# The output projection of each layer as one group of seven products

## The chip, the cores and the metric

The kernel runs on one core of a Trainium2 chip. The metric is the device time of one launch, in microseconds (us); the time given is the median of several runs.

## The reference, cut to what matters

Two layers of a hybrid decoder, on one sequence of 512 tokens with 1024 channels, all in float32. Each layer is a feed-forward, a mixer and a second feed-forward:

```python
for l in range(2):
    x = x + 0.5 * swiglu(rms_norm(x, ffn1_norm[l]), ffn1_wg[l], ffn1_wu[l], ffn1_wd[l])
    z = rms_norm(x, mix_norm[l]) @ w_in[l]       # q | k | v | conv_B | conv_C | conv_h
    attn_out = sliding_window_attention(q, k, v, sink[l])               # 512 channels
    conv_out = conv_B * causal_conv3(conv_C * conv_h, conv_w[l])        # 512 channels
    x = x + concat([attn_out, conv_out]) @ w_out[l]                     # 1024 x 1024
    x = x + 0.5 * swiglu(rms_norm(x, ffn2_norm[l]), ffn2_wg[l], ffn2_wu[l], ffn2_wd[l])
return rms_norm(x, final_norm)
```

The line with `w_out` is the output projection.

## The kernel before

The activations x lie in SBUF with channels on the partitions: eight tiles `xs[c]` of 128 channels by 512 tokens, in pairs `xpair` (the trace calls them x). TensorE (PE) multiplies in a rounded 32-bit form (`F32R`), so each operand is split into a rounded first part and a second part with the rest: `split` (lines 198 and 199) casts on ScalarE (ACT) and subtracts on VectorE (DVE). Each product is then three matmuls: first by first, first by second, second by first.

Weights come through one stream. `plan` writes out all units and the order of their use; `need_raw` loads units four ahead, through the queue of SyncE (SP), into 8 buffers `raw`; `need_split` splits them two ahead into 3 buffers `wh` and 3 buffers `wl`. A split marked "far" (lines 236 to 238) makes the second part without VectorE: ScalarE writes the negated rounded copy and the rounded copy, and a DMA issued by GpSimd (POOL) adds the raw tile to the negated copy. The scheduler of the language puts the instructions of each engine in order; each engine then works through its own in that order, and one that waits holds up all behind it.

Two ways to multiply are used:

- `group` (lines 258 to 276): a plain product, one tile of 128 output channels, 8 k-tiles with three matmuls of 512 columns each, 24 in all. The output projection uses eight of them, in `mix` (lines 1278 to 1281). After each, VectorE adds the result to `xs[c]`, and `after(c)` prepares the next norm for that tile: `take` makes its two parts (xh, xl), `square` adds to the sum of squares (nacc).
- groups of seven (Strassen's scheme in Winograd's form): a product of 2 by 2 blocks by seven products of half the size. The forms of the weights are a11, a12, s2, s3, s1, a22, s4; the operands are b11, b21, t2, t3, t1, t4, b22 in the order of `CHAINS`. `Seven.make` makes an operand (sums t1 to t4 on VectorE, then a split); `share` runs the seven products for a down projection, with `stand`, whose matmuls have 256 columns, and adds each result to the quarters of x that it belongs to (`SHARES`). Of the weight sums, s1 and s3 start in DRAM: a second load, issued by POOL, adds to the first as it lands (line 193). s2 is added on VectorE (line 217), and for units marked "share" s4 = a12 + s2 is a DMA issued by POOL (line 243). At the end of a feed-forward the last `share` calls `into.step` after each product, which calls `take_half` for that quarter of x, the counterpart of `take`.

The mixer (`mix`) runs 18 plain groups of `w_in` with the norm factored out; between them `attend(step)` puts the stages of eight attention units (two groups of heads by four blocks of 128 tokens): scores, transposes, values. The convolution multiplies on POOL, the last time `cb` by y. The outputs are split at once into the projection's operands `m`: for attention by ScalarE and POOL, for the convolution by ScalarE and VectorE.

Behind the mixer the second feed-forward begins with `plain`: four plain groups, with the inverse root of the norm worked out in the second (`factors`), then a small down projection, then blocks of seven products (`winograd2`, matmuls in `stream`).

Of the kernel before, what the change touches and what calls it, by code (L numbers as in the profile page):

```python
# [15 lines left out]
P = 128  # L16
# [42 lines left out]
def trunk_kernel(  # L59
# [32 lines left out]
    def psum(tag, shape, name):  # L92
        return ps.tile(shape, F32, tag=tag, bufs={"mm": 4, "sc": 2, "aux": 2}[tag], name=name)
# [21 lines left out]
    def f32(ap):  # L115
        return ap.bitcast(F32)
# [177 lines left out]
    def plan():  # L294
        def cols(src, k0, kc, n, how=None):
            wide = abreast(kc)
            for b in range(0, n, wide):
                order.append((add_unit((src, k0, kc, b * P, wide * P)), how))
# [349 lines left out]
    def make_bias():  # L648
# [9 lines left out]
        for h in range(NH):  # L658
            nc.vector.scalar_tensor_tensor(
                bias[:, h, :], df, -(2.0 ** -(h + 1)), m0, op0=ALU.mult, op1=ALU.add  # L660
            )


    def ffn(norm, stages, after=None, late=None):

# [167 lines left out]

            pending.extend(lambda *tag, c=c: turn(c, *tag) for c in range(NT))

        def stand(accs, wh, wl, xh, xl, h, start):

            for c in range(4):
                cols = slice(c * P, (c + 1) * P)
                for k in range(2):  # L840
                    for i, (w, x_) in enumerate(((wh, xh), (wh, xl), (wl, xh))):

                        nc.tensor.matmul(  # L843
                            accs[c // 2][:, c % 2, :],
                            w[:, k, cols],
                            x_[:, 2 * h + k, :],
                            start=start and c % 2 == 0 and h + k + i == 0,
                            stop=h + k == 2 and i == 2,
                            skip_group_check=True,
                        )  # L850

        def stream(accs, wh, wl, xh, xl, h, start):

            for u in range(2):
                tok = slice(u * P, (u + 1) * P)
                for k in range(2):
                    for i, (x_, w) in enumerate(((xh, wh), (xl, wh), (xh, wl))):
                        nc.tensor.matmul(  # L858
                            accs[u],
                            x_[:, 2 * h + k, tok],  # L860
                            w[:, k, :],
                            start=start and h + k + i == 0,
                            stop=h + k == 2 and i == 2,
                            skip_group_check=not start,
                        )

        def share(b, ops, between, y=None):


            accs = {}  # L870
            for step, (acc, operand, start) in enumerate(CHAINS):
                ops.make(operand)
                xh, xl = ops.forms[operand]
                if start:
                    tag = {"x": "mm", "y": "sc", "w": "aux"}[acc]
                    shape = [P, 2, H] if y is None else [P, S]
                    accs[acc] = [psum(tag, shape, f"{acc}_{ops.name}_{m}") for m in range(2)]
                o, t, sign = SHARES[step]
                for h in range(2):
                    _, wh, wl = take_split()  # L880
                    if y is None:
                        stand(accs[acc], wh, wl, xh, xl, h, start)
                    else:
                        stream(accs[acc], wh, wl, xh, xl, h, start)
                    if h == 0:
                        continue
                    for m in range(2):
                        if y is None:
                            part = xpair[2 * o + m][:, :, t * H : (t + 1) * H]
                        else:  # L890
                            part = y[2 * t + m][o]
                        nc.vector.scalar_tensor_tensor(
                            part, accs[acc][m], 0.5 * sign, part, op0=ALU.mult, op1=ALU.add
                        )
                if step < 3:
                    ops.make(CHAINS[step + 4][1])
                between(step)

        def shared(b):
            return Seven([raws[b], raws[b + 2]], room_form, f"s_{norm.i}_{b}")  # L900

        def turns(step):
# [2 lines left out]
                flush()  # L905
            if step == 2:
                flush(2, "mm")

        def ahead(ops, at):
            return lambda step: ops.make(*at.get(step, ()))  # L910

        sevens = [b for what, b in stages if what == "s"]
        blocks = [b + j for b in sevens for j in (0, 2)]
# [9 lines left out]
        for i, (what, b) in enumerate(stages):  # L923
            if what in "wu" and stages[i + 1][0] == "s":
                ops = shared(sevens[0])
                if what == "w":
                    winograd2(b, ahead(ops, {3: ("b11",), 4: ("b21",), 5: ("t2",), 6: ("t3",)}))
                else:
                    winograd(b, ahead(ops, {1: ("b11",), 2: ("b21",), 4: ("t2",), 6: ("t3",)}))
            elif what == "w":  # L930
                if after is None and b == 1:
                    end = Finale()
                winograd2(b, end and b == 1 and end.step)
            if what == "s" and b == sevens[0]:
                then = shared(sevens[1])
                share(
                    b,
                    ops,
                    ahead(then, {3: ("b11",), 4: ("b21",), 5: ("t2",), 6: ("t3",)}),
                    end and end.y,  # L940
                )
            elif what == "s" and i + 1 == len(stages):
                share(b, then, after.step)
            elif what == "s":
                share(b, then, lambda step: 2 <= step < 6 and flush(1, "aux"), end and end.y)
# [24 lines left out]
            if b == (1,) and late:  # L970
                late()
# [123 lines left out]


    def mix(l, norm, after):
        mixed = [None] * KC
        q = [None] * NH

        def scaled(acc, name, by=None):
            t = g2(name)
# [11 lines left out]
        for g in range(NKV):  # L1114
# [27 lines left out]
        class Unit:  # L1142
# [61 lines left out]
            def values(self):  # L1204
# [7 lines left out]
                    nc.tensor.matmul(o, v, lo, start=False, stop=i == len(self.pt) - 1)  # L1212
# [12 lines left out]

# [21 lines left out]
        for pair in range(2):  # L1247
# [6 lines left out]
            for j in range(2):  # L1254
# [11 lines left out]
                ys.append(y)  # L1266
                attend(step)
                step += 1
            hi, lo = parts_of(f"m_{l}_{2 + pair}")
            for j in range(2):  # L1270
                b = scaled(group(norm.h), f"cb_{l}_{pair}_{j}")
                nc.gpsimd.tensor_mul(b, b, ys[j])
                nc.scalar.copy(hi[:, j, :], b)
                nc.vector.tensor_sub(lo[:, j, :], b, f32(hi[:, j, :]))
# [63 lines left out]
```

## Time and profile before

| | |
|---|---|
| time, median of 3 runs | 1692.62 us (1692.27 to 1692.71) |
| the profiled execution | 1692.13 us, of it span 1690.3 us |
| mean granted TensorE clock | 0.999 |
| output projection, layer 0 | 470.2 to 513.7 us of the span |
| output projection, layer 1 | 1304.9 to 1348.5 us |

In the rows of the profile the engines are PE (matmuls), PEld (weight loads), DVE, ACT, POOL and SPq or POOLq for queues; "out<-in" names the tiles, L and a number is the line of the kernel, a bracket at the end is the idle time before an instruction and what ended it. A row of the timeline begins with the start in us from the start of the span and the length in us.

### The profile page before, as it was taken

What the parts mean: (1) busy time and instruction counts of PE and PEld (TensorE: products, weight loads), DVE (VectorE), ACT (ScalarE), POOL (GpSimd) and SP (SyncE); (2) the same over time, 40 slices, a digit from 0 to 9 for tenths busy, and PEclk for the clock granted to TensorE, in tenths of its full rate; (3) what the DMA queues carried; (4) which work ended last, traced back from release to release, by engine and by line L of the source; (5) the groups of instructions that cost most, each with busy time, mean ns of one, the idle gap of its engine ahead of it and who ended that gap; (6) DMA issues with size and microseconds to landing.
All of it is one profiled execution on the core that took longest, in us unless ns stands there. A gap on an engine that the chain in (4) does not pass through costs nothing.

```text
span 1690.3 us, 22800 instructions
## 1 busy us (share of the span) xinstructions
PE 1680.5 (99%) x8726; PEld 1434.4 (85%) x8726; DVE 1345.3 (80%) x1751; ACT 942.3 (56%) x1309; POOL 209.5 (12%) x190
## 2 busy tenths in 40 slices
PE   9999999999999999999999999999999999999998
PEld 6888899988888888889988888999888888888886
DVE  7987679988858976799798777997787597667995
ACT  6545565466535655564465555644565466556654
POOL 1011111001211111111011111110023011111111
PEclk9999999999999999999999999999999999999999
DMA  8467777731337677778576777794223457777881
GB/s 250 104 170 190 185 198 184 191 100 51 112 102 154 172 183 182 186 195 209 163 150 170 191 185 184 192 224 139 62 63 114 112 124 192 184 185 185 222 215 50
DMA packets 197600, 271.53 MB, mean 161 GB/s; under 512 B 8620, under 2 KB 91636, under 8 KB 197492
## 3 DMA queue, kind: packets, MB, share of 16 engines
q1 hardware_dynamic: 162308, 197.85, 37.5%
q0 software_dynamic: 34032, 70.79, 24.7%
q8 instruction: 68, 1.11, 0.3%
q10 hardware_dynamic: 1152, 1.45, 0.2%
q14 instruction: 40, 0.33, 0.1%
HBM read 254.85 MB, written 2.10 MB: 152 GB/s over the span
## 4 chain that ended last, share of the span: by engine, by line
PE 96%; DVE 2%; ACT 1%; DMA 0%; issue 0%; SPq 0%; ACTq 0%; DVEq 0%
PE x L858 24%; PE y L858 12%; PE acc L271 9%; PE acc L268 9%; PE acc L275 9%; PE x_s L843 8%; PE w L858 6%; PE y_s L843 4%; PE x_s L858 3%; PE w_s L843 2%; PE at L823 2%; PE y_s L858 1%; PE x L737 1%; PE w_s L858 1%; PE pt L1197 1%; DVE p L1190 0%
## 5 line engine op out<-in xcount | busy, mean ns | idle before, releaser
L198 ACT CAST wh<-raw 128x1024 fp32r<-128x1024 f32 (+1 forms) x472 | 494.7, 1048 | 552.7 <-PE x L858 134.2
L199 DVE TENSOR_TENSOR wl<-raw,wh 128x1024 fp32r<-128x1024 f32 (+1 forms) x471 | 578.5, 1229 | 214.5 <-ACT wh L198 212.5
L268 PE MATMUL acc<-xh,wh 128*128 128x512 f32 x448 | 176.5, 394 | 0.1
L271 PE MATMUL acc<-xl,wh 128*128 128x512 f32 x448 | 175.2, 391 | 0.1
L275 PE MATMUL acc<-xh,wl 128*128 128x512 f32 x416 | 162.4, 390 | 0.0
L193 POOL DMA_DIRECT2D raw<-in_ffn_wu_dram x39 | 47.3, 1217 | 569.1 <-DMA raw<-in_ffn_wu_dram 402.1
L271 PEld LDWEIGHTS acc<-xl,wh 128*128 128x128 f32 x448 | 84.2, 188 | 18.3 <-DVE xl L396 1.6
L268 PEld LDWEIGHTS acc<-xh,wh 128*128 128x128 f32 x448 | 84.2, 188 | 17.4 <-issue 0.5
L275 PEld LDWEIGHTS acc<-xh,wl 128*128 128x128 f32 x416 | 78.1, 188 | 16.3
L193 POOL DMA_DIRECT2D raw<-in_ffn_wg_dram x39 | 47.1, 1220 | 218.2 <-DMA raw<-in_ffn_wu_dram 70.9
L193 POOL DMA_DIRECT2D raw<-in_ffn_wd_dram x32 | 38.5, 1204 | 265.7 <-DMA raw<-in_ffn_wd_dram 144.8
L217 DVE TENSOR_TENSOR raw<-raw,raw 128x1024 f32<-128x1024 f32 x54 | 65.6, 1220 | 1.7 <-DMA raw<-in_ffn_wu_dram 1.0
L858 PE MATMUL w<-wh,fb21h 128*128 128x512 f32 x152 | 60.7, 399 | 0.0
L858 PE MATMUL x<-wh,ft2h 128*128 128x512 f32 x152 | 60.6, 398 | 0.0
L858 PE MATMUL y<-wh,ft3h 128*128 128x512 f32 x152 | 60.4, 398 | 0.0
L858 PE MATMUL w<-wl,fb21h 128*128 128x512 f32 x152 | 59.4, 391 | 0.0
L858 PE MATMUL x<-wl,ft2h 128*128 128x512 f32 x152 | 59.3, 390 | 0.0
L858 PE MATMUL y<-wh,ft3l 128*128 128x512 f32 x152 | 59.2, 390 | 0.0
L858 PE MATMUL y<-wl,ft3h 128*128 128x512 f32 x152 | 59.2, 390 | 0.0
L858 PE MATMUL w<-wh,fb21l 128*128 128x512 f32 x152 | 59.2, 389 | 0.0
L858 PE MATMUL x<-wl,fb11h 128*128 128x512 f32 x152 | 59.2, 389 | 0.0
L858 PE MATMUL x<-wh,fb11l 128*128 128x512 f32 x152 | 59.1, 389 | 0.0
(440 smaller groups left out, 4656.9 us busy)
## 6 DMA issues: line engine op xcount, KB each, us to landing
raw<-in_ffn_wu_dram SPq DMA_DIRECT2D x127, 512.0 KB, 4.0
raw<-in_ffn_wd_dram SPq DMA_DIRECT2D x104, 512.0 KB, 5.1
raw<-in_ffn_wg_dram SPq DMA_DIRECT2D x87, 512.0 KB, 4.5
raw<-in_ffn_wu_dram POOLq DMA_DIRECT2D x39, 512.0 KB, 7.9
raw<-in_ffn_wg_dram POOLq DMA_DIRECT2D x39, 512.0 KB, 5.9
raw<-in_w_in_dram SPq DMA_DIRECT2D x36, 512.0 KB, 3.7
raw<-in_ffn_wd_dram POOLq DMA_DIRECT2D x32, 512.0 KB, 8.1
raw<-raw POOLq DMA_DIRECT2D x16, 512.0 KB, 6.9
```

The costliest lines, as they stand in the source:

```text
L193: nc.gpsimd.dma_start(out=r, in_=rows_of(*more), accum_op=ALU.add)
L198: nc.scalar.copy(hi, raw)
L199: eng.tensor_sub(lo, raw, f32(hi))
L217: nc.vector.tensor_add(a11, a11, s1)
L268: nc.tensor.matmul(acc, hi[:, k, :], rhs[k][0], start=k == first, stop=False)
L271: nc.tensor.matmul(acc, hi[:, k, :], rhs[k][1], start=False, stop=n == 0 and k == last)
L275: nc.tensor.matmul(acc, lo[:, k, :], rhs[k][0], start=False, stop=k == last)
L737: nc.tensor.matmul(out, w[:, k, cols], x_[:, k, :], start=start and k + i == 0, stop=k == KC // 2 - 1 and i == 2, skip_group_check=not start,)
L823: nc.tensor.transpose(tp[:, t * P : (t + 1) * P], ups[t][:, c * P : (c + 1) * P], ident)
L843: nc.tensor.matmul(accs[c // 2][:, c % 2, :], w[:, k, cols], x_[:, 2 * h + k, :], start=start and c % 2 == 0 and h + k + i == 0, stop=h + ...
L858: nc.tensor.matmul(accs[u], x_[:, 2 * h + k, tok], w[:, k, :], start=start and h + k + i == 0, stop=h + k == 2 and i == 2, skip_group_chec ...
L1197: nc.tensor.transpose(tp[:, h, :], self.p[:, h, kb * P : (kb + 1) * P], ident)
```

## The change

`plan` puts `w_out` in as a group of seven instead of eight column units. Its tiles are marked "share", the very first "far". `stand`, `stream`, `share` and `ahead` move out of `ffn` unchanged but for two arguments of `share`: the factor `by` (0.5 in the feed-forwards, 1.0 here), and `soon`, with which the operand of the product after next is made ahead of the additions onto x. In `mix` the attention and the convolution write their outputs unsplit into `mixed[0]` and `mixed[1]` (attention and convolution channels); the very last multiplication by y goes to VectorE, and the eight groups with `after(c)` become one `share` with `after.step`. b11 is made after the last attention unit, b21 after the last convolution group.

```diff
-            cols(w_out[l], 0, KC, KC)
+            seven(
+                lambda o, j, h: (w_out[l], KC // 2 * j + 2 * h, 2, o * S, S),
+                lambda what, h: "far" if (what, h) == ("a11", 0) else "share",
+            )
...
+    def share(ops, by, between, y=None, soon=False):
...
+                if h == 0:
+                    continue
+                if soon and step + 2 < len(CHAINS):
+                    ops.make(CHAINS[step + 2][1])
...
-                            part, accs[acc][m], 0.5 * sign, part, op0=ALU.mult, op1=ALU.add
+                        part, accs[acc][m], by * sign, part, op0=ALU.mult, op1=ALU.add
...
-                if step < 3:
+            if not soon and step < 3:
                 ops.make(CHAINS[step + 4][1])
...
     def mix(l, norm, after):
-        mixed = [None] * KC
+        mixed = [g8(f"m_{l}_{j}", F32, (P, KC // 2, S)) for j in range(2)]
+        ops = Seven(mixed, room_g8, f"m_{l}")
...
-        amix = {}
-        for g in range(NKV):
-            h = parts_of(f"m_{l}_{g}")
-            amix[g] = h
-            for j in range(2):
-                mixed[2 * g + j] = (h[0][:, j, :], h[1][:, j, :])
...
-                f = g2(f"of_{self.name}", F32, (P, 2, P))
+                f = mixed[0][:, 2 * g : 2 * g + 2, n * P : (n + 1) * P]
...
-                mh, ml = (z[:, :, n * P : (n + 1) * P] for z in amix[g])
-                nc.scalar.copy(mh, f)
-                nc.gpsimd.tensor_sub(ml, f, f32(mh))
...
-            hi, lo = parts_of(f"m_{l}_{2 + pair}")
             for j in range(2):
                 b = scaled(group(norm.h), f"cb_{l}_{pair}_{j}")
-                nc.gpsimd.tensor_mul(b, b, ys[j])
-                nc.scalar.copy(hi[:, j, :], b)
-                nc.vector.tensor_sub(lo[:, j, :], b, f32(hi[:, j, :]))
-                mixed[4 + 2 * pair + j] = (hi[:, j, :], lo[:, j, :])
+                eng = nc.vector if pair and j else nc.gpsimd
+                eng.tensor_mul(mixed[1][:, 2 * pair + j, :], b, ys[j])
                 attend(step)
                 step += 1
-        for c in range(KC):
-            acc = group(mixed)
-            nc.vector.tensor_add(xs[c], acc, xs[c])
-            after(c)
+                if step == 17:
+                    ops.make("b11")
+        ops.make("b21")
+        share(ops, 1.0, after.step, soon=True)
```

More of the change, by code (lines that the diff above doesn't have):

```diff
@@ L661, in make_bias, with stand @@
             )
+    def stand(accs, wh, wl, xh, xl, h, start):
+        for c in range(4):
+            cols = slice(c * P, (c + 1) * P)
+            for k in range(2):
+                for i, (w, x_) in enumerate(((wh, xh), (wh, xl), (wl, xh))):
+                    nc.tensor.matmul(
+                        accs[c // 2][:, c % 2, :],
+                        w[:, k, cols],
+                        x_[:, 2 * h + k, :],
+                        start=start and c % 2 == 0 and h + k + i == 0,
+                        stop=h + k == 2 and i == 2,
+                        skip_group_check=True,
+                    )
@@ new lines, in stream @@
+    def stream(accs, wh, wl, xh, xl, h, start):
+        for u in range(2):
+            tok = slice(u * P, (u + 1) * P)
+            for k in range(2):
+                for i, (x_, w) in enumerate(((xh, wh), (xl, wh), (xh, wl))):
+                    nc.tensor.matmul(
+                        accs[u],
+                        x_[:, 2 * h + k, tok],
+                        w[:, k, :],
+                        start=start and h + k + i == 0,
+                        stop=h + k == 2 and i == 2,
+                        skip_group_check=not start,
+                    )
@@ L664, in ffn, with ahead @@
+    def ahead(ops, at):
+        return lambda step: ops.make(*at.get(step, ()))
     def ffn(norm, stages, after=None, late=None):
@@ L834, in winograd2 @@
             pending.extend(lambda *tag, c=c: turn(c, *tag) for c in range(NT))
[L836 to L892, printed above, removed]
-                            part, accs[acc][m], 0.5 * sign, part, op0=ALU.mult, op1=ALU.add
-                        )
-                if step < 3:
-                    ops.make(CHAINS[step + 4][1])
-                between(step)
@@ L907, in turns @@
                 flush(2, "mm")
-        def ahead(ops, at):
-            return lambda step: ops.make(*at.get(step, ()))
         sevens = [b for what, b in stages if what == "s"]
@@ L936, in ffn @@
                 share(
-                    b,
                     ops,
+                    0.5,
                     ahead(then, {3: ("b11",), 4: ("b21",), 5: ("t2",), 6: ("t3",)}),
@@ L942, in ffn @@
             elif what == "s" and i + 1 == len(stages):
-                share(b, then, after.step)
+                share(then, 0.5, after.step)
             elif what == "s":
-                share(b, then, lambda step: 2 <= step < 6 and flush(1, "aux"), end and end.y)
+                share(then, 0.5, lambda step: 2 <= step < 6 and flush(1, "aux"), end and end.y)
             if what == "p":
```

24 lines of the change are left out of this document (added).

## The prediction

> **What bounds the kernel now.** I read the page first: shares of the engines, then the chain that ended last.
>
> ```profile
> span 1690.3 us, 22800 instructions
> PE 1680.5 (99%) x8726; PEld 1434.4 (85%) x8726; DVE 1345.3 (80%) x1751; ACT 942.3 (56%) x1309; POOL 209.5 (12%) x190
> PE 96%; DVE 2%; ACT 1%; DMA 0%; issue 0%; SPq 0%; ACTq 0%; DVEq 0%
> ```
>
> TensorE (PE) is the bound, so fewer matmul columns are worth time as long as nobody else becomes late. But VectorE (DVE) is busy 80% on average, and an average hides stages. So I then asked for the busy time in stretches: the last block of seven products of the first feed-forward (309 to 349), the output projection of layer 0 (470 to 514), which is what is changed, and the stretch behind it. Columns: PE, PEld, DVE, ACT, POOL busy.
>
> ```profile
> 309.30:349.40 40.10, 40.10 (x336) 40.10 (x336) 36.09 (x51) 24.16 (x34) 1.76 (x2) 1.00 0.66 171
> ...
> 470.20:513.70 43.50, 43.50 (x193) 36.03 (x192) 25.31 (x30) 17.06 (x23) 2.68 (x3) 1.00 0.34 92
> ```
>
> The first row is a preview of the change: 336 matmuls of 256 columns from `stand`, with the next norm's `take_half` inside, and VectorE already busy 36.1 of 40.1 us. The projection as it is leaves VectorE 18 us idle.
>
> **The matmuls.** The projection has 8 groups of 24 matmuls of 512 columns; the changed one has 7 products of 48 matmuls of 256. The timeline of PE gives the ends of the old one (first matmul of it, first matmul behind it), the chain of waits one product of the new kind.
>
> ```profile
> 470.22 0.39 PE L268 MATMUL acc<-m,wh 128*128 128x512 f32 x1
> 513.74 0.39 PE L268 MATMUL acc<-xh,wh 128*128 128x512 f32 x1
> 343.84 5.76 PE x_s L843 x48
> ```
>
> Old: 513.74 - 470.22 = 43.52 us, 227 ns each. New: 7 x 5.76 = 40.32 us, 120 ns each. So PE saves 3.2 us in a layer, 6.4 in both, and no more: halving the columns does not halve the matmul. The Trainium skill, "TensorE: Matmul & The Clock Gate", section "Back-to-back issue gap", puts a warm stream at N/2.4 + 2.5 ns; by that (an estimate) 192 x 215.8 - 336 x 109.2 ns = 4.7 us would be saved in a layer, 9.5 in all. The rows have 227 and 120 ns where the page has 216 and 109, so the rows decide; and VectorE's load, next, would be the same.
>
> **VectorE in the new stage.** These are the prices, from start to start, since consecutive instructions overlap at their ends.
>
> ```profile
> 311.06 1.22 DVE L199 TENSOR_TENSOR wl<-raw,wh 128x1024 fp32r<-128x1024 f32 x1
> 312.20 1.22 DVE L510 TENSOR_TENSOR sum_s<-sum_s,raw_a 128x1024 f32<-128x1024 f32 x1
> 313.33 1.22 DVE L199 TENSOR_TENSOR wl<-raw,wh 128x1024 fp32r<-128x1024 f32 x1
> 314.47 1.30 DVE L892 SCALAR_TENSOR_TENSOR x<-x_s,x 128x512 f32<-128x512 f32 x2
> 315.68 1.22 DVE L199 TENSOR_TENSOR ft4l_s<-sum_s,ft4h_s 128x1024 fp32r<-128x1024 f32 x1
> 340.22 1.67 DVE L421 SCALAR_TENSOR_TENSOR xl<-x,par,xh 128x256 fp32r<-128x256 f32 x4
> 341.80 0.42 DVE L434 TENSOR_TENSOR nacc<-nsq 128x256 f32<-128x256 f32 x1
> 343.27 0.42 DVE L432 TENSOR_TENSOR nacc<-nacc,nsq 128x256 f32<-128x256 f32 x1
> 343.60 1.22 DVE L199 TENSOR_TENSOR wl<-raw,wh 128x1024 fp32r<-128x1024 f32 x1
> 470.42 0.69 DVE L1104 TENSOR_TENSOR cb<-acc,inv 128x512 f32<-128x512 f32 x1 [1.30 <-PE acc L275]
> ```
>
> A 128x1024 operation takes 1.135 us, one addition of a result onto x 0.605, an xl of 256 columns 0.40, a step of nacc 0.33. In the stage at 309 four operands were made ahead, in the block before. Here only b11 can be: b21 needs the last column group of the mixer, and t3, t2 need b21's neighbours, so they fall into the stage. The last row is the head: `cb` of the last group starts at 470.42, 0.2 us after PE begins the projection, and nothing but PE released it. From there to the first xl that closes the next norm (channels 0 to 3, second half of the tokens, which waits for the last product), VectorE has in its order: cb and the multiplication, 2 x 0.6; 14 second parts of weights, 6 of operands (b21, t2, t3, t1, t4, b22) and 4 operand sums, 24 x 1.135 = 27.2; 14 additions onto x, 8.5; 12 xl, 4.8; 10 of nacc, 3.3. Sum 45.0 us, and 0.5 for the xl itself: ready at 515.9 if VectorE never waits. It waits for ScalarE's casts in some four places; I put 0.1 to 0.3 us each, 0.8 in all (the row at 570.00 below shows 0.30), so 516.7.
>
> PE, unhindered, would end the products at 470.22 + 40.32 = 510.54 and want that xl at the 14th matmul of the next group, 510.54 + 13 x 0.227 = 513.5. It is late by 2.4 (no waits) to 3.6 us, I take 3.2: the whole saving of the layer. Some of it is paid earlier, at the second part of the weights of the last product, which stands behind 36 us of that work. Thereafter the inverse root of the norm waits for the same queue (five more nacc, two weight parts, the norm's split); the two matmuls that sum the squares wait some 0.2 us. Per layer: -3.2 + 3.2 + 0.2 = +0.2 us, and ±1.
>
> **In front of it.** The second part of the first weight tile goes by DMA, and the sum s2 overwrites that tile, so VectorE waits for this DMA; queued behind that wait are `cb` of the last but one group, the second tile's second part, an attention sum and the other s2.
>
> ```profile
> 435.32 0.50 PE L1212 MATMUL o<-pl,vv 128*128 128x512 f32 x1 [0.37 <-DVE pl L1201]
> 456.59 1.06 ACT L198 CAST wh<-raw 128x1024 fp32r<-128x1024 f32 x1 [1.00 <-PE acc L271]
> 457.68 1.23 DVE L199 TENSOR_TENSOR wl<-raw,wh 128x1024 fp32r<-128x1024 f32 x1
> 457.69 2.35 POOL L1257 TENSOR_TENSOR ch<-ch,cc 128x512 f32<-128x512 f32 x1 [0.56 <-DVE ch L1104]
> 463.05 1.29 DVE L1201 TENSOR_TENSOR pl<-pt,ph 128x512 fp32r<-128x512 f32 x2
> 467.98 0.69 DVE L1274 TENSOR_TENSOR m<-cb,m 128x512 fp32r<-128x512 f32 x1 [1.51 <-ACT m L1273]
> 471.26 1.29 POOL L1272 TENSOR_TENSOR cb<-cb,cc 128x512 f32<-128x512 f32 x1 [0.89 <-DVE cb L1104]
> ```
>
> And of the DMAs: those of line 238, issued by POOL, with their landing, and two rows of the page's part on issues.
>
> ```profile
> L238 POOL DMA_DIRECT2D wl<-raw x9: 852/889/901, 527.4 to 1373.0; - x9
> DMA to landing us min/median/max: 4.4/5.3/9.1
> ```
>
> ```profile
> raw<-in_ffn_wg_dram SPq DMA_DIRECT2D x87, 512.0 KB, 4.5
> raw<-raw POOLq DMA_DIRECT2D x16, 512.0 KB, 6.9
> ```
>
> The row at 456.59 is the cast of the first weight tile; the negated copy, of the same size, follows it on ScalarE, to 458.7. POOL has by then nearly finished its `ch` multiplication (1.3 us, as in the row at 471.26, once the split beside it at 457.68 is gone), so the DMA goes out at about 459.0 and lands, by the nine such DMAs of line 238, at 463.4 to 468.1, likeliest 464.3. VectorE gets there at 464.3, after the `pl` of the row at 463.05. Behind it lie 2 x 1.135 for the sums, 1.135, 0.6 and 0.8 = 4.8 us, to 469.1, and 470.42 is when `cb` can start: 1.3 us of slack, so nothing is paid while the DMA lands by 465.6. The removed splits of the mixer's outputs take 4 x 0.7 us off VectorE (row at 467.98), and some off ScalarE and POOL, that were hidden under PE; the split of b11 takes their place. The one wait of PE that they may have caused is the 0.37 us at 435.32, and there a split of weights moves ahead of the `pl` that PE waits for, so I leave it: zero, with 0.4 us either way.
>
> The seven weight tiles need ten buffers where there are eight, so the last two loads wait for the first two tiles, whose last reader is an s4 sum on POOL's DMA queue. The second goes out when the second product's weights are split, at about 477, and lands by the last row at 484; a load of 4.5 behind it is there at 488.5, against a need from 493 on, the sixth product's cast. Hidden by over 4 us. POOL's queue also has the four accumulating loads; those ahead of the conv multiplications wait for loads that went out 8 us and more before, so they hold nothing up.
>
> **Behind it.** VectorE was full behind the projection already, and this is where a backlog costs a second time. Two rows of VectorE and the chain of PE, first winograd block of the second feed-forward:
>
> ```profile
> 538.55 0.69 DVE L199 TENSOR_TENSOR a<-gate,a 128x512 fp32r<-128x512 f32 x1 [0.29 <-ACT a L198]
> 567.34 2.36 DVE L199 TENSOR_TENSOR wl<-raw,wh 128x1024 fp32r<-128x1024 f32 x2
> 570.00 1.23 DVE L199 TENSOR_TENSOR wl<-raw,wh 128x1024 fp32r<-128x1024 f32 x1 [0.30 <-ACT wh L198]
> 569.06 5.44 PE x L858 x24
> 1400.15 1.75 PE yt L992 x16
> ```
>
> From 538.55 VectorE has next to no idle time until 570.00. The first of the two parts at 567.34 is done at 568.5 and its product begins at 569.06, wanting it in the third matmul (569.5): 1.0 us of slack. After the change one sum of 1.135 us moves behind 538.55, and that point itself comes 0.2 later: 0.3 us paid in layer 0. In layer 1 PE has its transposes (last row) in this block, and more slack: nothing.
>
> Sum: 2 x 0.2 + 0.3 = +0.7 us, on the profiled execution's 1692.13 us (1.8 outside the span): 1692.8. The median of the runs, 1692.62, lies 0.5 above that execution; so 1693.3 for the median.
>
> **The rivals.** (A) PE's whole saving arrives: VectorE's load is no wall, and 6.4 us go: 1686.2. For it: PE is 99% busy and ended 96% of the chain. Against it: the row at 309.30 has 36.1 us of VectorE in 40.1, and the new stage adds b21, t3, t2 with their two sums (5 x 1.135) and the last cb and multiplication (1.2) to such a stage: 43.0, over 40.3, even before the end is looked at. It needs an order in which the closing xl comes before other work. Half of it would give 1689.5.
> (B) Slower: the DMA of the first tile's second part lands late. From 465.6 each us of delay moves VectorE's whole full stretch, and so PE, by one us in each layer. At 9.1 us (the slowest of the nine) it is 468.1: 2.5 us a layer, 1692.6 + 0.7 + 5.0 = 1698.3. It turns into over 0.2% from about 467.0. For it: the load and accumulating DMAs of other tiles fly at the same time. Against it: the median, 5.3. The multiplication left on POOL pushes the same way: beside the split at 457.68 POOL took 2.35 us where others take 1.3, and were it VectorE that is held, that is 1.1 us, still within the 1.3 of slack. The Trainium skill, "SBUF — State Buffer", section "SBUF: two separate sides", says that POOL and a VectorE operation with two SBUF inputs lock each other out of a shared port pair, whoever comes first; the two rows agree.
> (C) It does not do what it says: the sum for s4 and half of the loads' sums still go by POOL's DMA queue; as told, that is hidden, 1693.
>
> **How the numbers follow.** 0.2% (3.4 us) is about what a measurement of this kernel can tell from no change. My forecast 0.62, all of it within 0.2%; A 0.10, with a part of it (half the saving) 0.03 more that is also near the edge; B 0.18; the rest, 0.07, unforeseen waits, mostly slower. Faster 0.11, same 0.65, slower 0.24. The range takes the ±1 us a layer of the forecast and its cheap end, and B up to its worst row: 1689.5 to 1698.5; A lies outside it.
>
> **What would show it.** In the profile after: 672 matmuls of 256 columns at line 673 with 5.76 us for a product; VectorE over 95% busy from the start of the products to the next feed-forward's first group; PE idle there some 3 us in a layer, released by VectorE's `wl` of the last product and by ScalarE's or VectorE's xh, xl of channels 0 to 3; next to no wait of VectorE for the DMA at the first s2. I am wrong if PE runs through the stage without such waits (A), or if the first wait is at the second product, for b21 (B).

## The result and the profile after

The changed kernel takes 1695.99 us (median of 22 runs, 1694.39 to 1699.46), the one before 1692.59 (22 runs, 1692.04 to 1694.3): a ratio of 1.0021, with a 95% interval of 1.0014 to 1.0027. So it is 3.4 us slower, and the interval lies on both sides of the 0.2% that the prediction named as the edge of what can be told. The profiled execution took 1695.73 us, 3.60 more than the one before.

The page of the changed kernel, its span, engines and chain:

```profile
span 1694.0 us, 23555 instructions
PE 1678.3 (99%) x9014; PEld 1443.9 (85%) x9014; DVE 1388.8 (82%) x1823; ACT 962.6 (57%) x1329; POOL 207.9 (12%) x186
PE 89%; DVE 5%; DMA 2%; issue 2%; POOL 0%; ACT 0%; POOLq 0%; DVEq 0%; ACTq 0%; SPq 0%
```

TensorE is busy 2.2 us less, VectorE 43.5 us more, and TensorE's share of the chain fell from 96 to 89%. Busy time in stretches, first the seven products of layer 0 and then the stretch to the next feed-forward's down projection (columns as in the prediction):

```profile
470.50:513.00 42.50, 41.05 (x338) 40.55 (x337) 42.37 (x56) 27.52 (x37) 3.31 (x4) 1.00 0.67 172
513.00:538.30 25.30, 24.24 (x104) 18.67 (x102) 23.26 (x40) 19.12 (x26) 5.36 (x6) 1.00 0.81 188
```

VectorE is busy 42.37 of 42.5 us in the products. TensorE's waits there, from its timeline (the bracket is the wait and what ended it), with one in front and one far from the change:

```profile
457.50 0.50 PE L1213 MATMUL o<-pl,vv 128*128 128x512 f32 x1 [0.64 <-DVE pl L1202]
476.85 0.39 PE L673 MATMUL w_m<-fb21l_m,wh 128*128 128x256 f32 x1 [0.30 <-DVE fb21l_m L199]
507.54 0.39 PE L673 MATMUL x_m<-fb22h_m,wl 128*128 128x256 f32 x1 [1.15 <-DVE wl L199]
516.54 0.96 PE L268 MATMUL acc<-xh,wh 128*128 128x512 f32 x3 [0.73 <-ACT xh L423]
517.66 0.50 PE L271 MATMUL acc<-xl,wh 128*128 128x512 f32 x1 [0.16 <-DVE xl L424]
885.11 0.50 PE L688 MATMUL x<-wl,fb11h 128*128 128x512 f32 x1 [0.81 <-DMA wl<-raw]
```

From start to start, less the time of the matmul before, the four inside and just behind the stage are 0.46, 1.31, 0.88 and 0.44 us: 3.09 of the 3.2 that the matmuls save. VectorE in front of the stage, and the xl that closes the next norm:

```profile
459.35 0.89 POOL L238 DMA_DIRECT2D wl<-raw  x1
466.80 1.22 DVE L217 TENSOR_TENSOR raw<-raw,raw 128x1024 f32<-128x1024 f32 x1 [3.09 <-DMA wl<-raw]
471.91 0.68 DVE L1111 TENSOR_TENSOR cb<-acc,inv 128x512 f32<-128x512 f32 x1
517.13 0.48 DVE L424 SCALAR_TENSOR_TENSOR xl<-x,par,xh 128x256 fp32r<-128x256 f32 x1
```

The DMA part (the second part of the first weight tile, which a DMA makes) was issued at 459.35 and landed at 466.8; VectorE stood 3.09 us for it, and `cb` began at 471.91, 1.4 us after TensorE had begun the products at 470.51.

Set beside the trace of before, group by group, the time of the profiled execution was lost in four places: 0.22 us ahead of layer 0's mixer, 1.03 from there to the first winograd block (now at 548.38), 1.15 between 600 and 1190, nearly all of it at 885, and 1.24 around layer 1's projection.

### The profile page after: what moved, and what is told of

Read it like the earlier page. It is cut to its first block, busy times and chain, and to the rows that moved or that the text cites. A ratio compares the mean times of both kernels' runs of the same rounds, so it can differ in the third digit from the quotient of the medians.

```text
span 1694.0 us, 23555 instructions
## 1 busy us (share of the span) xinstructions
PE 1678.3 (99%) x9014; PEld 1443.9 (85%) x9014; DVE 1388.8 (82%) x1823; ACT 962.6 (57%) x1329; POOL 207.9 (12%) x186
## 4 chain that ended last, share of the span: by engine, by line
PE 89%; DVE 5%; DMA 2%; issue 2%; POOL 0%; ACT 0%; POOLq 0%; DVEq 0%; ACTq 0%; SPq 0%
PE x L688 24%; PE y L688 12%; PE x_s L673 8%; PE acc L271 6%; PE acc L268 6%; PE w L688 6%; PE acc L275 6%; PE y_s L673 4%; PE x_s L688 3%; PE w_s L673 2%; PE at L894 2%; DMA wl<-raw 2%; DVE wl L199 1%; PE y_s L688 1%; PE w_m L673 1%
## 5 line engine op out<-in xcount | busy, mean ns | idle before, releaser
L198 ACT CAST wh<-raw 128x1024 fp32r<-128x1024 f32 (+1 forms) x482 | 505.1, 1048 | 542.2 <-PE x L688 133.9
L199 DVE TENSOR_TENSOR wl<-raw,wh 128x1024 fp32r<-128x1024 f32 (+1 forms) x481 | 588.1, 1225 | 206.6 <-ACT wh L198 204.7
L217 DVE TENSOR_TENSOR raw<-raw,raw 128x1024 f32<-128x1024 f32 x58 | 71.0, 1229 | 9.6 <-issue 3.4
```

Source lines behind the costliest of these rows:

```text
L198: nc.scalar.copy(hi, raw)
L199: eng.tensor_sub(lo, raw, f32(hi))
L217: nc.vector.tensor_add(a11, a11, s1)
```

## The experiments

Theory V: from the first product to the next norm VectorE's queue is full, and each us of work in it, or of lateness ahead of it, is a us of TensorE. Its first rival is that the landing of the DMA part alone sets the loss; the second, that it comes from elsewhere. Theory F is about the wait at 885 alone: a fetch of code, a packet of the queue q8 (kind "instruction"), runs beside a copy and makes it late. All times are medians; the kernel before stood at 1692.3 to 1692.8 beside them.

**1. No DMA part.**

```diff
-                lambda what, h: "far" if (what, h) == ("a11", 0) else "share",
+                lambda what, h: "share",
```

> Edit: the second part of the first weight tile is made on VectorE like all others, not by a DMA; nothing else. In the profile after, VectorE stood 3.09 us at the first s2 sum for that DMA and made cb of the last mixer group 1.4 us late. Theory V with landing (VectorE is the wall, and the late landing adds to it): the 3.09 us go, 1.135 us of split come, cb is in time; the wait at the second product (0.46 us) goes and the end of the stage comes 1.0 to 1.4 us earlier in each layer: 1693.0 to 1694.2 against 1696.0, and a smaller spread of the runs. Rival W (only the amount of VectorE work counts, the DMA's landing does not): 1.135 us more work in each layer, 1697 to 1698.5. Rival S (the losses come from elsewhere, from the shared transfers): unchanged, 1696.

1693.41 us (1692.54 to 1696.38; ratio to before 1.0008, 0.9999 to 1.0017): 2.6 less than the changed kernel, and in the range of V with landing. The spread did not shrink clearly. VectorE, then TensorE:

```profile
470.42 0.69 DVE L1111 TENSOR_TENSOR cb<-acc,inv 128x512 f32<-128x512 f32 x1 [2.09 <-PE acc L275]
506.38 0.39 PE L673 MATMUL x_m<-fb22h_m,wl 128*128 128x256 f32 x1 [0.97 <-DVE wl L199]
515.39 0.50 PE L268 MATMUL acc<-xh,wh 128*128 128x512 f32 x1 [0.72 <-ACT xh L423]
```

`cb` again starts when TensorE lets it, after 2.09 us of idle time: there is room for the split that came back. The wait at the second product is gone, those at the end stay, and so does TensorE's wait for `a`, which now stands at 537.15 instead of 538.26 us. Of these 1.1 us the profiled execution had gained 0.5 in the first 8 us of the program, where the edit does not reach, and 0.6 from there on; layer 1 gained 0.9, and another 1.1 is the wait at 885, which is not there either (experiment 11 says why). So the DMA part cost 0.6 and 0.9 us in the two layers of this execution, less than V's 1.0 to 1.4, and the time is in V's range with the help of the wait at 885, which V did not count. The full queue is a loss of its own.

**2. The DMA part for a12 instead of a11.**

```diff
-                lambda what, h: "far" if (what, h) == ("a11", 0) else "share",
+                lambda what, h: "far" if (what, h) in (("a12", 0),) else "share",
```

> Edit: the second part that goes by DMA is that of a12's first tile (second product) in place of a11's first tile. No sum overwrites a12 before the fourth product, so VectorE waits for no landing there, and it has 1.135 us less to do than with no DMA part. Theory V with landing: 1.0 us better in each layer than without the DMA part, 1691.0 to 1693.0. Rival: the landing only moves to TensorE, which needs this part 6 us after the first product's start; the copy that the DMA adds to can begin only when a buffer comes free some 5 us before that start, so a landing of 7 us or more after the issue is waited for by TensorE: 1694 to 1697 with a wide spread.

1705.68 us (ratio 1.0076, 1.0064 to 1.0089): the rival's case, and worse than its range. ScalarE, POOL and TensorE:

```profile
470.61 1.05 ACT L237 CAST wh<-raw 128x1024 fp32r<-128x1024 f32 x1 [4.65 <-PE acc L271]
471.57 1.05 ACT L236 ACTIVATE wl<-raw 128x1024 fp32r<-128x1024 f32 x1
472.06 1.21 POOL L193 DMA_DIRECT2D raw<-in_w_out_dram  x1 [4.36 <-DMA raw<-in_w_out_dram]
472.92 1.26 POOL L238 DMA_DIRECT2D wl<-raw  x1
480.71 0.38 PE L673 MATMUL w_m<-fb21h_m,wl 128*128 128x256 f32 x1 [3.92 <-DMA wl<-raw]
```

ScalarE's two copies stood 4.65 us for a buffer that TensorE freed at 470.6, as the rival had it; the negated copy was done at 472.62 and the DMA went out at 472.92. The accumulating load ahead of it in POOL's queue had itself waited 4.36 us for the load that it adds to, but that held the DMA up by 0.3 us only. It then landed in 7.75 us, beside that load, when TensorE had stood for it 3.92 us; in layer 1 it was 4.89. The matmuls behind these waits also run at 0.21 us each instead of 0.12; more on that at the end.

**3. Twelve of fourteen nacc additions left out,** so that the norm's sum of squares is incomplete.

```diff
+                if t in self.begun and self.i % 3 == 2:
+                    continue
                 if t in self.begun:
                     nc.vector.tensor_add(acc, acc, sq[:, 0])
```

> Edit: of the 14 additions of squares (nacc, 0.33 us each) of the norm behind each output projection the 12 accumulating ones are left out, which leaves that norm's sum of squares incomplete; the DMA part stays. Theory V (VectorE's queue is full from the first product to the next norm): 8 of them stand before the closing xl, 2.6 us, so the waits at the last product's second weight part (1.3 us) and at xh and xl (1.3 us) go: 4 to 5 us less in all, 1691.0 to 1692.2. Rival (the landing of the DMA alone sets the loss, VectorE having room behind it): less than 1 us, 1695 to 1696.

1690.27 us (1688.74 to 1692.82; ratio 0.9989, 0.9980 to 0.9997): 5.7 less than the changed kernel, more than V asked for, although the wait at 883 is 2.25 us here: in the two layers the profiled execution gained 6.2. The rival falls. The DMA part is still late, and TensorE still waits for b21; but the last product has no wait left, and from 511 to 537 TensorE is busy throughout:

```profile
476.83 0.39 PE L675 MATMUL w_m<-fb21l_m,wh 128*128 128x256 f32 x1 [0.45 <-DVE fb21l_m L199]
505.85 0.28 PE L675 MATMUL x_m<-fb22h_m,wl 128*128 128x256 f32 x1
511.00:537.00 26.00, 26.00 (x115) 20.79 (x114) 23.80 (x35) 20.01 (x27) 6.17 (x6) 1.00 0.83 189
```

**4 and 5. The change in one layer alone.** The old projection is kept in the other layer (`if l in NEW: ... else:` around the lines of the diff).

> Edit: the change is made in layer 0 alone; layer 1 has the old projection. The profile after lost 1.25 us around the projection of layer 0, 1.29 around that of layer 1, and 1.0 at 885 us, in the first feed-forward of layer 1, where TensorE waited for a DMA part though no code of that place was changed. If that wait follows from the change ahead of it (loads shifted by two buffers): 1694.5 to 1695.0, with the wait at 885 in the profile. If it is a landing of chance or belongs to the execution: 1693.7 to 1694.1, without it.

> Edit: the change in layer 1 alone; layer 0 has the old projection. With the change in layer 0 alone 2.4 us were lost, 1.2 of them at 885 us, where TensorE waited for a DMA part whose forerunner landed in 6.1 us instead of 4.7: one packet of an instruction queue ran on one of the DMA engines beside it. Theory F (the changed layer 0 has 144 more matmuls, so the fetch of code falls at another place): with layer 0 as before, the code up to 885 is as before, no instruction packet beside that DMA part, no wait, and only the 1.2 to 1.4 us around layer 1's projection are lost: 1693.7 to 1694.1. Rival (the wait is there by chance of the execution): a wait at 883 also here, 1694.7 to 1695.2.

Layer 0 alone: 1695.0 us (ratio 1.0014, 1.0005 to 1.0023), with a wait of 1.21 us at 885.82. Layer 1 alone: 1694.8 (1.0012, 1.0003 to 1.0021), with none there, and the part ahead of it landing in 4.8 us. So the wait at 885 follows layer 0's change. The time of layer 1 alone is above its forecast and within the range of the rival, but the rival's wait is not in the trace: the kernel's own DMA part landed in 8.7 us instead of 7.7, and TensorE stood about 1 us longer for b21:

```profile
wl<-raw POOLq DMA_DIRECT2D x1, 512.0 KB, 8.7
1312.63 0.39 PE L677 MATMUL w_m<-fb21l_m,wh 128*128 128x256 f32 x1 [1.64 <-DVE fb21l_m L200]
```

**6. The last multiplication back on POOL.**

```diff
-                eng = nc.vector if pair and j else nc.gpsimd
+                eng = nc.gpsimd
```

> Edit: of the change alone the last multiplication is undone: cb_1_1 is multiplied on POOL as the other three are; the DMA part stays. It takes 0.6 us off VectorE in each layer, but the second operand b21 and the sum t3 then wait for POOL's 1.3 to 2.2 us in place of 0.6. Theory V: b21 is 0.7 to 1.6 us later, while VectorE can take other parts in the meantime: the wait at the second product grows from 0.46 and 0.81 us to 1 to 2, the later ones shrink by as much or less: 1696 to 1698. Rival (VectorE's work alone counts): 0.6 us less in each layer, 1694.8.

1696.88 us (1695.17 to 1697.96; ratio 1.0022, 1.0012 to 1.0033): within V's range, and not told apart from the changed kernel. VectorE idles at the head (first row) and TensorE waits later for a second part (second row). So the multiplication on VectorE neither pays nor costs anything that shows.

```profile
474.60 1.22 DVE L508 TENSOR_TENSOR sums_m<-m,m 128x1024 f32<-128x1024 f32 x1 [1.18 <-POOL m L1270]
513.75 0.50 PE L275 MATMUL acc<-xh,wl 128*128 128x512 f32 x1 [0.97 <-DVE wl L199]
```

**7. The nacc additions on POOL.**

```diff
-                    nc.vector.tensor_add(acc, acc, sq[:, 0])
-                    nc.vector.tensor_add(acc, acc, sq[:, 1])
+                    eng = nc.gpsimd if self.i % 3 == 2 else nc.vector
+                    eng.tensor_add(acc, acc, sq[:, 0])
+                    eng.tensor_add(acc, acc, sq[:, 1])
```

> Edit: the 12 accumulating nacc additions, left out in the other run, are made on POOL, idle in this stretch (3.3 of 42.5 us). If POOL's work beside VectorE costs nothing: as with the additions left out, 1690 to 1691. If the two hold each other up on additions of two SBUF tiles, as the rows of the mixer suggest (POOL's multiplication 2.2 to 2.35 us beside a split where it takes 1.3 alone, VectorE's split 1.9 where it takes 1.2): at two thirds of a us for one of 256 columns on POOL, 12 of them take 8 us of the port from VectorE where they took 4.0: 1697 to 1701, and the norm's sum of squares is late too.

1702.86 us (ratio 1.0060, 1.0046 to 1.0073), above the range named. POOL, VectorE and TensorE:

```profile
514.53 1.59 POOL L435 TENSOR_TENSOR nacc<-nacc,nsq 128x256 f32<-128x256 f32 x1
516.20 0.73 POOL L436 TENSOR_TENSOR nacc<-nacc,nsq 128x256 f32<-128x256 f32 x1
513.78 1.75 DVE L199 TENSOR_TENSOR wl<-raw,wh 128x1024 fp32r<-128x1024 f32 x1
524.91 0.59 PE L465 MATMUL ssq<-sqh,ones_r 128*128 128x512 f32 x1 [2.63 <-ACT sqh L198]
526.15 0.63 PE L268 MATMUL acc<-xh,wh 128*128 128x512 f32 x1
```

TensorE waits 2.63 us for the sum of the squares (2.69 in layer 1), and the split beside POOL's addition takes 1.75 us for 1.22. The Trainium skill, "SBUF — State Buffer", section "SBUF: two separate sides", has POOL and a VectorE operation of two SBUF inputs locking each other out; the pair 1.59 against 0.73 and 1.75 against 1.22 agrees. So POOL's idle time was no place for this work.

**8. Two operand sums by DMA,** on top of experiment 1.

```diff
                     nc.vector.tensor_sub(t3, b12, b22)
+                    if self.dma:
+                        nc.scalar.activation(b12, b12, AF.Copy, scale=-1.0)
+                        nc.gpsimd.dma_start(out=b12, in_=b11, accum_op=ALU.add)
...
-                if what == "t1":
+                if what == "t1" and not self.dma:
                     nc.vector.tensor_sub(b12, b11, b12)
-                if what == "t4":
+                if what == "t4" and not self.dma:
                     nc.vector.tensor_add(self.sums[1], self.sums[1], b21)
...
                 split(hi, lo, src)
+                if what == "t2" and self.dma:
+                    nc.gpsimd.dma_start(out=self.sums[1], in_=b21, accum_op=ALU.add)
```

> Edit, on top of the kernel without the DMA part: the operand sums t1 (b12 negated by ScalarE, then b11 added by DMA) and t4 (b21 added by DMA onto t2) leave VectorE, 2 x 1.135 us in each layer, all in the stretch from the first product to the closing xl. Theory V (VectorE's amount of work there is the wall): the waits at the last product (1.1 to 1.3 us) and at xh and xl (1.3) go nearly all, 2.0 to 2.3 us in each layer: 1688.8 to 1690.0 against 1693.4, so faster than both kernels. Rival D (the sums land late: the split of t1 stands in VectorE's queue for a landing, as s2 did): 1692 to 1696. Rival W570 (VectorE is full up to 570 us anyway, so TensorE pays there what it saves): 1692 to 1693.

1695.73 us (ratio 1.0017, 1.0008 to 1.0026), 2.3 more than without this: rival D, but by another engine than it named. The sum for t4 landed in 9.2 us; ScalarE's cast of t4 waited 3.35 us for it, and the cast of the next weights stood behind, so VectorE had nothing to split for 2.31 us:

```profile
480.53 1.28 POOL L523 DMA_DIRECT2D sums_m<-m  x1 [2.72 <-DVE ft2l_m L199]
489.73 1.05 ACT L198 CAST ft4h_m<-sums_m 128x1024 fp32r<-128x1024 f32 x1 [3.35 <-DMA sums_m<-m]
491.75 1.22 DVE L199 TENSOR_TENSOR wl<-raw,wh 128x1024 fp32r<-128x1024 f32 x1 [2.31 <-ACT wh L198]
```

What VectorE saved, 2 x 1.135 us, it lost there. In layer 1 the same sum landed in 11.0 us, and a wait of 1.56 us stood at 885.

**9. t1 before the stage,** on top of experiment 1, and **10. a fused last multiplication,** on top of 9.

```diff
+                    if self.early:
+                        nc.vector.scalar_tensor_tensor(
+                            t2, b12, -1.0, b22, op0=ALU.mult, op1=ALU.subtract
+                        )
+                        nc.vector.tensor_add(t3, t2, b11)
...
-                if what == "t1":
+                if what == "t1" and not self.early:
                     nc.vector.tensor_sub(b12, b11, b12)
...
                 if step == 17:
                     ops.make("b11")
+                    b11, b12 = mixed[0][:, :, :H], mixed[0][:, :, H:]
+                    nc.vector.tensor_sub(b12, b11, b12)
```

```diff
+                if pair and j:
+                    nc.gpsimd.tensor_mul(ys[j], ys[j], norm.inv)
+                    nc.vector.tensor_mul(mixed[1][:, 2 * pair + j, :], group(norm.h), ys[j])
+                else:
+                    b = scaled(group(norm.h), f"cb_{l}_{pair}_{j}")
+                    nc.gpsimd.tensor_mul(mixed[1][:, 2 * pair + j, :], b, ys[j])
```

> Edit, on top of the kernel without the DMA part: the sum t1 = b11 - b12, which needs only the attention's half of the mixer, is made before the last cb, where VectorE has 2.1 us idle in that kernel (before 470.42); t2 is then -t1 - b22 and t3 is t2 + b11, as many instructions as before. So 1.135 us leave the full stretch from the first product to the closing xl, without a DMA to wait for. Theory V (VectorE's work in that stretch is the wall): 1.0 to 1.1 us less in each layer, 1690.8 to 1691.6 against 1693.4, the wait at the last product going from 1.1 to 1.3 to about 0.1. Rival T (only the last part of the stretch counts, since the weights can be split no more than two tiles ahead, as in the run with the sums by DMA, which gained nothing from 2.3 us): 1693 to 1694, with an idle VectorE in the middle.

> Edit, on top of e9: of the last column group, cc is multiplied by inv on POOL while TensorE still computes, so the result is made by one VectorE instruction of TensorE's sum and that product, in place of two; 0.6 us less for VectorE in each layer, right at the head of the full stretch. Theory V: 0.5 to 0.6 us less in each layer than e9, 1689.6 to 1690.6. Rival T: as e9. Rival P (POOL's extra multiplication, 1.3 to 2.2 us, holds VectorE up beside it or is late): 0.5 to 1.5 us more than e9.

Nine: 1691.48 us (1690.74 to 1693.34; ratio 0.9995, 0.9987 to 1.0004), as V has it, though a wait of 1.05 us stood at 883. Ten: 1691.19 (1690.23 to 1695.25; ratio 0.9996, 0.9988 to 1.0005), 0.3 less where V asked for 1.0 to 1.2. The first two rows are nine's VectorE (the sum t1 ahead of `cb`), the others ten's TensorE:

```profile
468.37 1.21 DVE L1283 TENSOR_TENSOR m<-m 128x1024 f32<-128x1024 f32 x1
470.50 0.69 DVE L1118 TENSOR_TENSOR cb<-acc,inv 128x512 f32<-128x512 f32 x1 [0.92 <-PE acc L275]
506.73 0.28 PE L680 MATMUL x_m<-fb22h_m,wl 128*128 128x256 f32 x1
511.91 0.50 PE L275 MATMUL acc<-xh,wl 128*128 128x512 f32 x1 [0.48 <-DVE wl L199]
```

The sum fills most of the idle time that experiment 1 had opened, and the last product has no wait in either. What is left lies behind it. Ten misses V's forecast: in layer 0 both profiled kernels begin the first winograd block at the same time, and no run settles why. Both versions are 4.5 to 4.8 us below the changed kernel and some 1 us below the one before, but that last difference their intervals don't separate from none.

**11. The code shifted.** The changed kernel with 16 matmuls of 2 columns at its start, and two fewer of the idle ones.

```diff
-    spin(WARM)
+    spin(1)
+    for _ in range(16):
+        nc.tensor.matmul(idle[:, :2], zero[:, :P], zero[:, :2], start=True, stop=True)
```

> Edit: the changed kernel with 16 more matmuls of 2 columns at its very start and 2 of the 512-column idle ones there left out, so that all later code of TensorE lies 28 instructions further on. Nothing else. In the profile after, a packet of the instruction queue q8 ran at 460, at 865 and at 1296 us, each while a DMA part was in flight; these parts landed in 7.4, 6.0 and 7.7 us. 28 instructions are some 3.2 us of TensorE, so the packets should come about 3.2 us earlier, at 457, 862 and 1293, before these parts start. Theory F (code fetches beside the copies make them late): the parts land in 5 to 6 us, the wait at 885 goes (1.0 us), VectorE's wait of 3.1 us at the first s2 sum falls to 1 or 2 and the stage comes 0.5 to 1.2 us earlier in each layer: 1693 to 1694.5, with at most 0.7 us more at the start. Rival (the other loads in flight make them late, and the packets only lie beside them): landings and time as after, 1696 to 1696.7.

1694.64 us (1693.75 to 1697.85; ratio 1.0016, 1.0007 to 1.0025): 1.35 less, with no wait at 885. The view of DMAs from the issue of the part at 863 on, 6.2 us in 40 slices, and its landing: the changed kernel, then the shifted one.

```profile
DMA  0000000009696969696969696110101010100000
q8 instruction: 1, 0.02, 1.7%
wl<-raw POOLq DMA_DIRECT2D x1, 512.0 KB, 6.0
```

```profile
DMA  0000000009997979797979696100000000069965
q0 software_dynamic: 144, 0.52, 42.7%
wl<-raw POOLq DMA_DIRECT2D x1, 512.0 KB, 4.5
```

In the changed kernel one packet of the instruction queue q8 ran from 865.4 to 867.0, inside the copy; the slices of one tenth at the end of its strip fit one DMA engine that still had something to move. In the shifted kernel that packet ran at 862.1, ahead of the copy, which ended 1.6 us sooner. How a copy at 863 makes TensorE wait at 885 stands in POOL's queue (two rows of the changed kernel, one of the shifted):

```profile
876.41 1.21 POOL L193 DMA_DIRECT2D raw<-in_ffn_wg_dram  x1 [6.14 <-DMA raw<-in_ffn_wu_dram]
877.13 1.42 POOL L238 DMA_DIRECT2D wl<-raw  x1
872.38 1.21 POOL L195 DMA_DIRECT2D raw<-in_ffn_wg_dram  x1 [2.12 <-DMA raw<-in_ffn_wu_dram]
```

A load on SP's queue goes out 0.05 us after the landing. In the changed kernel it went out at 870.00, behind POOL's next DMA part (869.41), and took 5.8 us; in the shifted one at 868.42, ahead of that part, and took 3.4. The accumulating load that adds to it waited as much longer, and a third DMA part, which ScalarE had made ready at 874.55 in both kernels, stood behind it in POOL's queue: issued at 877.13 instead of 874.84, it landed at 885.06 instead of 883.01.

The thirteen profiled kernels agree. In ten a packet of q8 ran inside the copy at 863, and it landed in 5.6 to 6.3 us; in the other three (before, layer 1 alone, shifted) in 4.5 to 4.8. In the seven where it took 5.8 us or more, the load behind it took 5.8 to 6.1 and TensorE waited; in the other six, experiment 1 with 5.64 among them, the load took 3.4 to 4.4 and TensorE did not. So theory F holds at 885.

At the projection it does not: in layer 1 the packet moved to 1294.0, ahead of the issue at 1294.91, and the part still landed in 7.4 us. In layer 0 the packet hardly moved (459.9 for 460.3) and stayed beside the part, which took 7.7 us, so that layer says nothing.

## Why the prediction was right, and where its size was off

The range (1689.5 to 1698.5) held, and the ratio of 1.0021 lies at the edge between no difference and slower, the two cases that had 0.89 of the chance. The forecast was 1693.3, the median 1695.99: 2.7 us more, about 1 of it for the wait at 885 and most of the rest for the late landing, 1.5 in the two layers of experiment 1. By the prediction's own signs this was its forecast with rival B, which had 0.18 of the chance, on top: the first wait of the stage is for b21, and VectorE stood 3.09 us at the first s2, where next to nothing was to show. B's rule, a us in each layer for each us past 465.6, gives 1692.6 + 0.7 + 2 x 1.2 = 1695.7 for a landing at 466.8. That this is so near the median is luck: the landing cost some 1.5 us and not 2.4, and 1 us of the median is the wait at 885, which no term had. By its steps:

**The matmuls.** Held. The seven products took 42.40 us, of which 0.46 and 1.31 are waits: 40.63 against 40.32. The saving that the prediction works out from the Trainium skill, 4.7 us in a layer, did not come. (The section named there has its formula for a single matmul; for back-to-back matmuls the page has it in part 1.)

**The VectorE wall.** Held closely. From `cb` to the closing xl the sum was 45.0 us, 45.5 with the xl itself; the rows give 517.13 + 0.40 - 471.91 = 45.6. The 0.8 us for ScalarE's casts did not come, as VectorE never idled. TensorE paid 2.63 us at the weight part of the last product and at xh and xl of the norm, as forecast, and 0.46 at the second product for b21, which the prediction had named as the sign of rival B. That VectorE's work is the cause is shown by experiments 3 and 9.

**In front of it.** This term was mis-sized: "likeliest 464.3" for the landing, with 1.3 us of slack. The DMA went out at 459.35, as worked out to 0.4 us, but took 7.4 us instead of 5.3: it landed at 466.8, past the bound of 465.6, so rival B's mechanism ran alongside the forecast, at 0.6 and 0.9 us in the two layers (experiment 1). The median of 5.3 us was the middle of three kinds that the trace of before holds, three DMAs each: 4.4 to 4.7 us with no load beside them, 5.2 to 5.5 beside 0.52 MB of loads, 8.4 to 9.1 beside such loads and another 0.5 MB by POOL's queue. Around the new one 0.95 MB of loads moved in the same 8 us:

```profile
q1 hardware_dynamic: 498, 0.95, 40.9%
q0 software_dynamic: 144, 0.52, 33.1%
wl<-raw POOLq DMA_DIRECT2D x1, 512.0 KB, 7.4
```

In seven profiled kernels with the part in this place it landed in 6.9 to 8.7 us, where the one at 863 landed in 4.5 to 4.8 with neither a load nor a packet of q8 beside it. That the loads are the cause is argued from these bytes; no run took them away.

**Behind it.** The place was wrong, and the mechanism too. The 0.3 us in the winograd block did not come; TensorE stood 0.63 us at the matmuls of `a` one stage earlier, in layer 1 as in layer 0. TensorE, then VectorE:

```profile
538.26 0.50 PE L271 MATMUL acc<-a,wh 128*128 128x512 f32 x1
536.92 0.69 DVE L754 TENSOR_TENSOR gate<-acc,gate 128x512 f32<-128x512 f32 x1 [0.34 <-PE acc L275]
```

No backlog was left there: VectorE idled 0.34 us for TensorE and made this `gate` before it split `a`, of which ScalarE had the first part ready at 536.46. Experiments 1 and 9, which reach this place 1.1 and 2 us sooner, have the same 0.63 us. So it looks like the order of VectorE's instructions; no run changed that alone.

**Not seen at all.** The wait at 885, some 1 us: with 144 more matmuls in layer 0 the packet of q8 ran at 865.4 instead of 873.1, inside a copy in layer 1.

The sum for layer 0 by the named waits: -3.20 + 3.09 + 0.63 at `a`, and 0.15 for the wait that moved from 435.32 to 457.50, make +0.67 of the 1.03; the rest is made of gaps under 0.15 us, 0.31 of it within the seven products. Rival A fell; C did not show: `s4`'s sum goes by DMA, and nothing waits for it.

## What to carry to other kernels

Before a stage is given fewer matmuls, add up what the engine that feeds it has to do from its last free moment to the first operand behind the stage: here that sum was right to 0.1 us and took back the whole saving. A DMA in place of an engine's instruction has to be priced by the traffic in its own place, not by a median over places, and when it is late, all that stands behind the waiting instruction in that engine's queue is late with it. What helped was work moved into idle time just ahead of the full stretch (experiment 9), without a DMA to wait for.

## What the runs showed of the hardware

A fetch of code delays a copy beside it: with one packet of the queue q8 inside, a copy of 512 KB landed in 5.6 to 6.3 us (ten traces), without one in 4.5 to 4.8 (three), and a change of 28 instructions moved the packet out of the way.

After the four longest waits here TensorE ran at half speed for a while. Behind those of 2.63 and 2.69 us in experiment 7 the matmuls of 512 columns came every 0.43 us instead of 0.227; behind those of 3.92 and 4.89 us in experiment 2 the ones of 256 columns every 0.21 instead of 0.12. The granted clock was 0.50 for some 3.4 us each, and 6.8 with the longest. A wait of 2.25 us, at 883 in experiment 3, had no such tail. The granted clock, the last but two of the columns, for a stretch of experiment 7 and one of experiment 2, each partly outside the slow part:

```profile
524.90:528.00 3.10, 3.08 (x8) 2.44 (x9) 0.71 (x2) 2.01 (x3) 0.00 (x0) 0.55 1.07 269
```

```profile
483.00:486.00 3.00, 3.00 (x21) 3.00 (x21) 0.00 (x0) 0.93 (x1) 0.00 (x0) 0.75 1.12 218
```

The Trainium skill, "TensorE: Matmul & The Clock Gate", part 1, has the clock fall to half after an idle window of about 3.4 us, in windows that run freely; here 2.63 us were enough, and the measurement decides. That it falls to half agrees (granted clock 0.50).
